# RWKV-7 scans of a two-layer trunk: 17 instead of 9 columns of each block inverse on VectorE, its second pair of copies on VectorE, and a new order of the parts around them

## The chip, the cores and the metric

One core of one Trainium2 chip runs the whole program. The metric is the device time in microseconds. The kernel before took 1643.92 us, the median of three runs (1643.02 to 1644.35).

## The reference, cut to what matters

The program computes two residual layers over 512 tokens of width 1024: layer 0 with windowed attention, layer 1 with RWKV-7 time mixing, each followed by a convolutional feed-forward network. The change touches the time mixing of layer 1 alone, of which the reference says:

```python
def step(state, inp):
    r_t, w_t, k_t, v_t, a_t, b_t = inp
    sa = jnp.einsum('bhvk,bhk->bhv', state, a_t)
    state = state * w_t[:, :, None, :] + sa[..., None] * b_t[:, :, None, :] + v_t[..., None] * k_t[:, :, None, :]
    y = jnp.einsum('bhvk,bhk->bhv', state, r_t)
    return state, y
...
y = y_f + y_b                       # a forward and a backward scan
mean = jnp.mean(y, axis=-1, keepdims=True)
var = jnp.mean(jnp.square(y - mean), axis=-1, keepdims=True)
yn = ((y - mean) * lax.rsqrt(var + RWKV_GN_EPS)).reshape(b, s, d) * lnx_w + lnx_b
out = (yn + (bonus_f + bonus_b).reshape(b, s, d)) * g
```

There are 16 heads of 64 channels. The kernel does the scans in 8 chunks of 64 tokens, and inside a chunk it needs the inverse of a triangular 64x64 matrix for each head, direction and chunk.

## The kernel before, in words

The heads go in 8 pairs (`ct`, 0 to 7). Before the scans' own stretch the projections write each pair's operands to DRAM (`ars`, `bks`, ...). `run` (line 1209 on) then goes through i = -1 to 7, and in each i through 8 chunks j. At each j it writes down the parts that the string `K.between[j]` (line 1314) names, in that order: `c` is the scan step of pair i, and the other letters are parts for pairs ahead of it or behind it (`PARTS`, line 1188). At the end every instruction is tied to the one written before it on its engine, so that each engine's order is the order in which the parts stand in these strings. Each engine takes its instructions strictly in that order, and what one instruction waits for also holds those behind it.

What one pair needs, and which letters stand for it:

- `l0` to `l3` (`low`): matmuls, then a masked copy on VectorE (L936) into `bw`, for pair i+2. `b0` and `b1` (`blocks`): the 32x32 diagonal blocks go to DRAM (`ls`, two DMAs for each direction, L942, queue SP), and with `b1` they all come back as the tile X (L947, two DMAs).
- `G`, `V`, `g`, `v` with a number n (`go`, which advances `solve`): n more of the 31 columns of the inverse of these blocks, for pair i+2 (capitals) or i+1 (small letters). A column is a product (`tg` or `tv`, L997) and an addition into Y (L999); G and g put both on GpSimd (POOL), V and v on VectorE (DVE). Each column reads the ones before it, so they follow each other whatever engine they are on. Columns run from 31 down to 1, with 31 elements in a partition at first, 136 in the middle (column 17) and 16 at the end.
- After column 1, the 32nd advance copies Y into a tile Z in two orders, `z1` (a transposed one, two copies) and `z0` (two copies), and three DMAs on ACT's queue store them to `zs`: two for z1 and one for z0. Z and X are taken from one ring of four tiles (`block`).
- `I` (`inverses`), pair i+1: `zs` comes back as `t32` and `tt` (six DMAs on SP). `L0`, `L1` (`level`) complete the inverses; `L1` ends in four small copies into `tt`.
- `t`, `a`, `x`, `m`, `u`, `w`: transposes, products, loads of the values. `m` ends in the tiles `mt` and `qt` (L1080, L1081 on DVE).
- `n0` to `n4` (`head_norm`) for pair i-1: `n1` has a power on POOL (L1142, `rv`), `n2` is one multiplication (L1144), `n3` transposes on PE, and `n4` is two operations of 512 elements on DVE (L1152 and L1153), the second of which also multiplies by the gate `gt`. Then the result is stored (`os`, L1157). `e` loads `gt` and `bo`, `p` loads a later pair's `bk` and `ar`.

Before the change a pair's 31 columns stand as 4 on POOL (j3), 5 and 4 on DVE (j4, j5), 4 and 4 on POOL (j6, j7), and, in the next i, 5 and 5 on POOL (j0, j1) with the copies. The first pair is inverted by POOL alone inside the projections, and seven pairs are left for this scheme.

A DMA signals one of eight semaphores, DMAHW0 to DMAHW7. They are given out in turn to the DMAs of both queues together, in the order in which the program was put down, and a DMA is not issued before the DMA eight places earlier, on the same semaphore, has landed. Below, this is called its lane.

Of the kernel before, what the change touches and what calls it, by code (L numbers as in the profile page):

```python
# [16 lines left out]
P = 128  # L17
# [5 lines left out]
HD = 64  # L23
# [792 lines left out]
def rwkv_scan(K, A, sc, mid):  # L816
# [4 lines left out]
    V = nc.vector  # L821
# [25 lines left out]
    def mk(shape, name, bufs=1, dt=F32):  # L847
        pool = mid if name in MID else pools[next((k for k, v in PLACE.items() if name in v), "batch")]
        return pool.tile(shape, dt, name=name, tag=name, bufs=bufs)
# [47 lines left out]
    def eng(name, i=0):  # L897
        x = K.eng.get(f"{name}/{K.ct}", K.eng[name])
        return {"V": V, "G": G, "C": C, "A": nc.any, "S": nc.sync}[x[i % len(x)]]

    def copy(name, i, out, in_):
        e = eng(name, i)
        if e is C:
            C.copy(out=out, in_=in_)  # L904
        else:
            e.tensor_copy(out=out, in_=in_)
# [72 lines left out]
    def block():  # L979
        R.nX += 1  # L980
        return R.Xs[R.nX % len(R.Xs)]

    def solve(ct, c):


        X = c.X
        Y = mk([P, 32, 16], f"Y{ct % K.ny}")
        Yf = Y.rearrange("p i j -> p (i j)")
        G.memset(Y, 0.0)
        G.memset(Yf[0:HD, 0::33], 1.0)  # L990
        G.memset(Yf[HD:P, 16::33], 1.0)
        for kx in range(31, 0, -1):
            en, nm = (G, "tg") if c.by == "G" else (V, "tv")
            m = kx // 2
            n = 16 - m
            tm = mk([P, 256], nm, 1)[:, 0:kx * n].rearrange("p (i j) -> p i j", j=n)
            en.tensor_tensor(out=tm, in0=X[:, 0:kx, kx:kx + 1].broadcast_to([P, kx, n]),  # L997
                             in1=Y[:, kx:kx + 1, m:16].broadcast_to([P, kx, n]), op=ALU.mult)
            en.tensor_tensor(out=Y[:, 0:kx, m:16], in0=Y[:, 0:kx, m:16], in1=tm, op=ALU.add)  # L999
            yield  # L1000
        Z = block()
        for h in range(2):
            yh = Y[HD * h:HD * h + HD]
            copy("z1", h, Z[HD:P].rearrange("p (j h) i -> p j h i", h=2)[:, :, h], yh.rearrange("p i j -> p j i"))
        for h in range(2):
            yh = Y[HD * h:HD * h + HD]
            copy("z0", h, Z[0:HD].rearrange("p i (j h) -> p i j h", h=2)[:, :, :, h], yh)
        zd = sc["z"][ct]
        for d in range(2):
            nc.scalar.dma_start(out=zd[0, 48 * d:48 * d + 16], in_=Z[HD + 48 * d:HD + 48 * d + 16])  # L1010
        nc.scalar.dma_start(out=zd[1], in_=Z[0:HD])

    def go(ct, c, n, by):

        c.by = by
        if not hasattr(c, "solving"):
            c.solving = solve(ct, c)
        for _ in range(n):
            next(c.solving, None)
# [241 lines left out]
def body(ctx, tc, A, out, stage=9):  # L1261
    nc = tc.nc
    K = Ctx()
# [46 lines left out]
    K.eng.update({"w": "VC", "bkt": "C", "bkt/0": "C", "x1": "C", "xa": "C", "xv": "C", "z1": "C", "Q": "C"})  # L1310
    K.begin, K.tail = (2,), ("pl", "", "", "")
    K.ny = 2
    K.eng["tt"] = "CV"
    K.between = ("w0 c l0 l1 b0 u g5", "c l2 l3 g6 b1 I", "c m1 w1 n0 e", "c t0 t1 n1 G4", "c a0 p V5 n2", "c L0 n3 V4", "c L1 a1 n4 G4", "c x0 x1 m0 G4")
    const = ctx.enter_context(tc.tile_pool(name="const", bufs=1, reuse_waits="tile"))

    @contextmanager
# [54 lines left out]
    def ffn(layer, xT, st, nxt, nst, store):  # L1372
# [4 lines left out]
    sc = {"ar": dram.tile([KT, 2, P, 2, NC, HD], F32, name="ars"), "bk": dram.tile([KT, 2, P, NC, 2, HD], F32, name="bks"),  # L1377
          "v": dram.tile([S, D], F32, name="vs"), "g": dram.tile([KT, P, S], F32, name="gs"),
          "bo": dram.tile([KT, P, S], F32, name="bos"), "o": dram.tile([KT, P, S], F32, name="os"),
          "l": dram.tile([KT, 2, 2, NC, 2, 32, 32], F32, name="ls"), "z": dram.tile([KT, 2, HD, 32, 32], F32, name="zs")}  # L1380
# [22 lines left out]
    with ExitStack() as end:  # L1403
# [25 lines left out]
        for ot, (hi, lo) in enumerate(ahead(K, [(A["wo"][i], n * P, nc.vector) for i in range(KT)])):  # L1429
            ps = scan.bank()  # L1430
            for kt in range(n):
                c = slice(kt * P, (kt + 1) * P)
# [4 lines left out]
        with tc.tile_pool(name="act2", bufs=1, reuse_waits="tile") as K.act:  # L1437
            K.accp = K.work = K.act
            on_tile = residual(xT, "nch1" if stage > 2 else None, st if stage > 2 else None, out if stage == 2 else None)
            for ot in range(KT):  # L1440
                ps = scan.bank()
                c = slice(ot * P, (ot + 1) * P)
# [82 lines left out]
```

## Time and profile before

| | us |
|---|---|
| median of three runs | 1643.92 |
| profiled execution, its own time | 1642.19 |
| span of that execution in the trace | 1640.4 |
| stretch of the scans, about | 907 to 1180 |
| PE busy in the span | 1476.3 (90%) |
| DVE busy | 1006.3 (61%) |
| ACT busy | 683.5 (42%) |
| POOL busy | 491.8 (30%) |

The shares are means over stages with different limits. PE is full in the attention and in both feed-forward networks; in the scans it is not. A timeline row gives start, length, engine, line, operation, tiles with their sizes, and in brackets the idle time of the engine ahead of it with what ended it. `xN` says that N instructions were merged into a row. Start times count from the beginning of the span.

### The profile page before, as it was taken

What the parts mean: (1) busy time and instruction counts of PE and PEld (TensorE: products, weight loads), DVE (VectorE), ACT (ScalarE), POOL (GpSimd) and SP (SyncE); (2) the same over time, 40 slices, a digit from 0 to 9 for tenths busy, and PEclk for the clock granted to TensorE, in tenths of its full rate; (3) what the DMA queues carried; (4) which work ended last, traced back from release to release, by engine and by line L of the source; (5) the groups of instructions that cost most, each with busy time, mean ns of one, the idle gap of its engine ahead of it and who ended that gap; (6) DMA issues with size and microseconds to landing.
All of it is one profiled execution on the core that took longest, in us unless ns stands there. A gap on an engine that the chain in (4) does not pass through costs nothing. (4 is left out here: it accounts for less than half of the span.)

```text
span 1640.4 us, 28397 instructions
## 1 busy us (share of the span) xinstructions
PE 1476.3 (90%) x11612; PEld 1191.6 (73%) x11612; DVE 1006.3 (61%) x1570; ACT 683.5 (42%) x1131; POOL 491.8 (30%) x645
## 2 busy tenths in 40 slices
PE   8999999999999998989975867667769999999999
PEld 7767688888888886667754756556647788888887
DVE  6876448777763349959886444555356677777222
ACT  5576434444432224665534333333423444444211
POOL 2630012223300016435696444444300233222000
PEclk9999999999999999999975687888979999999999
DMA  5200032332233322356546356554443232333341
GB/s 190 78 21 1 27 90 90 103 101 92 91 115 100 119 78 90 100 156 246 189 158 183 121 122 135 149 143 88 116 144 97 74 94 90 103 101 91 105 119 61
DMA packets 108978, 179.09 MB, mean 109 GB/s; under 512 B 49200, under 2 KB 62128, under 8 KB 108848
## 3 DMA queue, kind: packets, MB, share of 16 engines
q1 hardware_dynamic: 107552, 174.13, 35.0%
q10 hardware_dynamic: 1296, 3.15, 0.9%
q8 instruction: 91, 1.49, 0.4%
q14 instruction: 39, 0.32, 0.1%
HBM read 142.91 MB, written 34.34 MB: 108 GB/s over the span
## 5 line engine op out<-in xcount | busy, mean ns | idle before, releaser
L68 ACT CAST whi<-wraw 128x1024 fp32r<-128x1024 f32 (+2 forms) x196 | 200.3, 1023 | 270.5 <-PE mm L105 182.1
L104 PE MATMUL mm<-hl,whi 128*128 128x512 f32 x720 | 281.7, 391 | 1.5 <-DVE xT L1355 0.9
L106 PE MATMUL mm<-hl,wlo 128*128 128x512 f32 x720 | 281.6, 391 | 0.5 <-POOL wlo L71 0.4
L105 PE MATMUL mm<-hl,whi 128*128 128x512 f32 x720 | 281.4, 391 | 0.4 <-DVE hl L92 0.4
L71 DVE TENSOR_TENSOR wlo<-wraw,whi 128x1024 fp32r<-128x1024 f32 (+2 forms) x139 | 167.7, 1207 | 182.6 <-ACT whi L68 181.8
L71 POOL TENSOR_TENSOR wlo<-wraw,whi 128x1024 fp32r<-128x1024 f32 x57 | 137.0, 2404 | 414.4 <-ACT whi L68 414.4
L185 DVE SCALAR_TENSOR_TENSOR conv<-upad,par,conv 128x512 f32<-128x512 f32 x88 | 125.6, 1429 | 64.0 <-ACT conv L182 64.0
L106 PEld LDWEIGHTS mm<-hl,wlo 128*128 128x128 f32 x720 | 135.6, 188 | 31.9 <-POOL wlo L71 2.7
L104 PEld LDWEIGHTS mm<-hl,whi 128*128 128x128 f32 x720 | 135.8, 189 | 29.6 <-ACT hl L91 1.3
L105 PEld LDWEIGHTS mm<-hl,whi 128*128 128x128 f32 x720 | 135.8, 189 | 29.5 <-DVE hl L92 1.1
L106 PE MATMUL mm<-gh,wlo 128*128 128x512 f32 x352 | 139.0, 395 | 0.0
L104 PE MATMUL mm<-gh,whi 128*128 128x512 f32 x352 | 139.0, 395 | 0.0
L105 PE MATMUL mm<-gl,whi 128*128 128x512 f32 x352 | 139.0, 395 | 0.0
L997 POOL TENSOR_TENSOR tg<-X,Y 128x56 f32<-128x56 f32 (+20 forms) x185 | 70.4, 381 | 93.4 <-DVE Y L999 42.8
L97 ACT CAST gh<-gact 128x512 fp32r<-128x512 f32 x44 | 27.3, 621 | 141.4 <-DVE gact L194 141.4
L999 POOL TENSOR_TENSOR Y<-Y,tg 128x56 f32<-128x56 f32 (+20 forms) x185 | 77.6, 420 | 13.3
L182 ACT ACTIVATE conv<-upad,par 128x512 f32<-128x512 f32 x88 | 71.6, 815 | 21.5 <-DVE upad L180 21.3
L105 PEld LDWEIGHTS mm<-gl,whi 128*128 128x128 f32 x352 | 66.1, 188 | 16.1
L106 PEld LDWEIGHTS mm<-gh,wlo 128*128 128x128 f32 x352 | 66.1, 188 | 16.0
L104 PEld LDWEIGHTS mm<-gh,whi 128*128 128x128 f32 x352 | 66.1, 188 | 16.0
L187 DVE SCALAR_TENSOR_TENSOR conv<-upad,par,conv 128x512 f32<-128x512 f32 x88 | 70.1, 798 | 3.0
L192 ACT ACTIVATE silu<-conv 128x512 f32<-128x512 f32 x44 | 27.8, 632 | 91.2 <-DVE conv L187 91.2
(336 smaller groups left out, 3068.8 us busy)
## 6 DMA issues: line engine op xcount, KB each, us to landing
wraw<-in_w_up_dram SPq DMA_DIRECT2D x88, 512.0 KB, 3.6
wraw<-in_w_down_dram SPq DMA_DIRECT2D x32, 512.0 KB, 3.5
ars<-tab SPq DMA_DIRECT2D x16, 512.0 KB, 2.9
bks<-tab SPq DMA_DIRECT2D x16, 512.0 KB, 3.5
ar<-ars SPq DMA_DIRECT2D x8, 1024.0 KB, 8.4
bk<-bks SPq DMA_DIRECT2D x8, 1024.0 KB, 6.7
wraw<-in_w_down_dram SPq DMA_DIRECT2D x16, 384.0 KB, 3.1
wraw<-in_w_qkv_dram SPq DMA_DIRECT2D x11, 512.0 KB, 4.1
```

The costliest lines, as they stand in the source:

```text
L68: nc.scalar.copy(out=hi, in_=raw)
L71: lo_engine.tensor_tensor(out=lo, in0=raw, in1=hi.bitcast(F32), op=ALU.subtract)
L97: K.nc.scalar.copy(out=hi, in_=src)
L104: nc.tensor.matmul(ps, lhsT=lhs[0], rhs=rhs[0], start=first, stop=False)
L105: nc.tensor.matmul(ps, lhsT=lhs[0], rhs=rhs[1], start=False, stop=False)
L106: nc.tensor.matmul(ps, lhsT=lhs[1], rhs=rhs[0], start=False, stop=last)
L182: nc.scalar.activation(out=c, in_=u[:, 1:S + 1], func=AF.Identity, scale=K.par[:, cw + 2 * FT + ch:cw + 2 * FT + ch + 1], bias=K.par[:, cb ...
L185: nc.vector.scalar_tensor_tensor(out=c, in0=u[:, 0:S], scalar=K.par[:, cw + ch:cw + ch + 1], in1=c, op0=ALU.mult, op1=ALU.add)
L187: nc.vector.scalar_tensor_tensor(out=c, in0=u[:, 2:S + 2], scalar=K.par[:, cw + 4 * FT + ch:cw + 4 * FT + ch + 1], in1=c, op0=ALU.mult, op ...
L192: nc.scalar.activation(out=sg, in_=acts[0], func=AF.Silu)
L997: en.tensor_tensor(out=tm, in0=X[:, 0:kx, kx:kx + 1].broadcast_to([P, kx, n]), in1=Y[:, kx:kx + 1, m:16].broadcast_to([P, kx, n]), op=ALU. ...
L999: en.tensor_tensor(out=Y[:, 0:kx, m:16], in0=Y[:, 0:kx, m:16], in1=tm, op=ALU.add)
```

## The change

Three things change:

- `solve` takes a tile for z1, makes its two copies and issues their two stores, and only then takes a further tile for z0. z0's copies move from ACT to DVE (`K.eng["z0"]`).
- The override that gave every second one of the four `tt` copies of `L1` to DVE goes, and all four are on ACT.
- The strings of `K.between` change: `b1` stands ahead of the part that ends the inverse of pair i+1; the columns of a pair are now 3 on POOL (j3), 6, 6 and 5 on DVE (j4 to j6), 4 on POOL (j7), and 4 and 4 on POOL in the next i; and `n2`, `n3` and `n4` stand ahead of the columns of their chunk.

```diff
+        zd = sc["z"][ct]
         Z = block()
         for h in range(2):
-            yh = Y[HD * h:HD * h + HD]
-            copy("z1", h, Z[HD:P].rearrange("p (j h) i -> p j h i", h=2)[:, :, h], yh.rearrange("p i j -> p j i"))
-        for h in range(2):
-            yh = Y[HD * h:HD * h + HD]
-            copy("z0", h, Z[0:HD].rearrange("p i (j h) -> p i j h", h=2)[:, :, :, h], yh)
-        zd = sc["z"][ct]
+            copy("z1", h, Z[HD:P].rearrange("p (j h) i -> p j h i", h=2)[:, :, h], Y[er(h)].rearrange("p i j -> p j i"))
         for d in range(2):
             nc.scalar.dma_start(out=zd[0, 48 * d:48 * d + 16], in_=Z[HD + 48 * d:HD + 48 * d + 16])
+        Z = block()
+        for h in range(2):
+            copy("z0", h, Z[0:HD].rearrange("p i (j h) -> p i j h", h=2)[:, :, :, h], Y[er(h)])
         nc.scalar.dma_start(out=zd[1], in_=Z[0:HD])
...
-    K.eng["tt"] = "CV"
-    K.between = ("w0 c l0 l1 b0 u g5", "c l2 l3 g6 b1 I", "c m1 w1 n0 e", "c t0 t1 n1 G4", "c a0 p V5 n2", "c L0 n3 V4", "c L1 a1 n4 G4", "c x0 x1 m0 G4")
+    K.eng["z0"] = "V"
+    K.between = ("w0 c l0 l1 b0 u g4", "c l2 l3 b1 g4 I", "c m1 w1 n0 e", "c t0 t1 n1 G3", "c a0 p n2 V6", "c L0 n3 V6", "c L1 a1 n4 V5", "c x0 x1 m0 G4")
```

Lines from 1011 on stand one line higher after the change (L1144 becomes L1143), and the stores of z1 stand at L1006 instead of L1010.

Which lane each store takes is in the order of the two programs. At the end of the inverse of one pair (i = 1; the others are like it), ACT's queue has before, from the first copy of z1 to the square of the norm:

```order
L904 COPY X1_7484<-Y1_8643 64x16x32
L904 COPY X1_7484<-Y1_8643 64x512 [waits DMAHW4_49]
L904 COPY X1_7484<-Y1_8643 64x512
L1010 DMA zs_78<-X1_7484 16x1024 [waits DMAHW5_49,Activation_49]
L1010 DMA zs_78<-X1_7484 16x1024 [waits DMAHW6_49]
L1011 DMA zs_78<-X1_7484 64x1024 [waits DMAHW7_49,Activation_49]
L1137 ACTIVATE t_9180<-t_9178 128x512 [waits DVE_49]
```

The copies of z0 (64x512) are the second kind, and the stores hold lanes 5, 6 and 7. After the change the same place on ACT reads:

```order
L904 COPY X0_5953<-Y1_8643 64x16x32
L1006 DMA zs_78<-X0_5953 16x1024 [waits DMAHW5_49,Activation_49]
L1006 DMA zs_78<-X0_5953 16x1024 [waits DMAHW6_49]
L1010 DMA zs_78<-X1_7484 64x1024 [waits DMAHW6_49,DMAHW4_49,DVE_49]
L1136 ACTIVATE t_9180<-t_9178 128x512 [waits DVE_49]
```

The stores of z1 hold lanes 5 and 6, and the store of z0 waits for DVE's copies and takes lane 6 after the second of them. SP's queue at the same place, before, with the blocks of the next pair (L942), its values (L955) and X (L947):

```order
L942 DMA ls_77<-bw1_7305 32x16x32 [waits DMAHW0_49,DVE_49]
L942 DMA ls_77<-bw1_7305 32x16x32 [waits DMAHW1_49]
L955 DMA vv_9037<-vs_73 64x8x128 [waits DMAHW2_49,PE_49,Activation_49]
L955 DMA vv_9037<-vs_73 64x4x128 [waits DMAHW3_49]
L955 DMA vv_9037<-vs_73 64x4x128 [waits DMAHW4_49]
L942 DMA ls_77<-bw1_7305 32x16x32 [waits DMAHW5_49,DVE_49]
L942 DMA ls_77<-bw1_7305 32x16x32 [waits DMAHW6_49]
L947 DMA X2_7485<-ls_77 64x1024 [waits DMAHW5_49,DMAHW6_49,DMAHW1_49,DMAHW7_49,DMAHW0_49,Pool_49]
```

And the same piece of SP's queue after the change:

```order
L942 DMA ls_77<-bw1_7305 32x16x32 [waits DMAHW7_49,DVE_49]
L942 DMA ls_77<-bw1_7305 32x16x32 [waits DMAHW0_49]
L955 DMA vv_9046<-vs_73 64x8x128 [waits DMAHW1_49,PE_49,Activation_49]
L955 DMA vv_9046<-vs_73 64x4x128 [waits DMAHW2_49]
L955 DMA vv_9046<-vs_73 64x4x128 [waits DMAHW3_49]
L942 DMA ls_77<-bw1_7305 32x16x32 [waits DMAHW4_49,DVE_49]
L942 DMA ls_77<-bw1_7305 32x16x32 [waits DMAHW5_49]
L947 DMA X3_7486<-ls_77 64x1024 [waits DMAHW5_49,DMAHW7_49,DMAHW4_49,DMAHW0_49]
```

The last two stores of blocks waited for lanes 5 and 6 and X for lane 7, which are the three stores to `zs`; now the first of the two is on lane 4, the second is still on lane 5, and X waits for no store of `zs`.

On DVE, the end of a pair's columns (j5 and j6) before, where `st` is the scan step:

```order
L999 TENSOR_TENSOR Y_9241<-Y_9241,tv 128x19x7
L1115 TENSOR_TENSOR st<-bank,gc 128x128
L906 COPY tt_7307<-mm 32x8x32 x2
L1152 SCALAR_TENSOR_TENSOR t<-bank,par,bo 128x512
L1153 TENSOR_TENSOR t<-t,gt 128x512
L1080 TENSOR_TENSOR mt_9502<-mm,id_5026 128x4x64
```

and the same place after:

```order
L999 TENSOR_TENSOR Y_9241<-Y_9241,tv 128x17x8
L1114 TENSOR_TENSOR st<-bank,gc 128x128
L1151 SCALAR_TENSOR_TENSOR t<-bank,par,bo 128x512
L1152 TENSOR_TENSOR t<-t,gt 128x512
L997 TENSOR_TENSOR tv<-X_7486,Y_9241 128x128
L999 TENSOR_TENSOR Y_9241<-Y_9241,tv 128x16x8
L997 TENSOR_TENSOR tv<-X_7486,Y_9241 128x135
```

The `tt` copies are gone from DVE, and the two operations of `n4`, which stood behind DVE's last column, now stand between its 12th and its 13th. At the change of pairs (j1) the copies of z0 now stand on DVE between the last masks and the scan step:

```order
L936 TENSOR_TENSOR bw_7483<-pre_5949,mask 128x4x128
L936 TENSOR_TENSOR bw_7483<-mm,mask 128x4x128 x2
L906 COPY X_5953<-Y_9241 64x512 x2
L1114 TENSOR_TENSOR st<-bank,gc 128x128
L1079 TENSOR_TENSOR mt_9536<-pre_5948,id_5026 128x4x64
```

Before, the scan step followed the masks directly. PE's order is the same in both programs.

## Rows read from the trace of the kernel before

**Rows 1.** Stretch: us, busy PE, PEld, DVE, ACT, POOL (count), granted clock, DMA share, GB/s.

```profile
1040.00:1080.00 40.00, 27.68 (x798) 24.51 (x792) 21.20 (x56) 14.66 (x32) 19.63 (x52) 0.87 0.53 127
```

**Rows 2.** Timeline of POOL over one pair: start, length, line, operation, idle before.

```profile
1032.07 0.42 POOL L997 TENSOR_TENSOR tg<-X,Y 128x126 f32<-128x126 f32 x1 [6.30 <-DVE Y L999]
...
1039.59 0.41 POOL L997 TENSOR_TENSOR tg<-X,Y 128x121 f32<-128x121 f32 x1
...
1048.22 0.22 POOL L999 TENSOR_TENSOR Y<-Y,tg 128x16 f32<-128x16 f32 x1
...
1061.29 0.25 POOL L997 TENSOR_TENSOR tg<-X,Y 128x31 f32<-128x31 f32 x1 [4.65 <-DMA X<-ls]
...
1063.38 0.28 POOL L997 TENSOR_TENSOR tg<-X,Y 128x56 f32<-128x56 f32 x1
...
1070.33 0.43 POOL L997 TENSOR_TENSOR tg<-X,Y 128x126 f32<-128x126 f32 x1 [6.29 <-DVE Y L999]
```

**Rows 3.** Timeline of ACT at the same change of pairs.

```profile
1048.48 2.87 ACT L904 COPY X<-Y 64x512 f32<-64x512 f32 x3 [7.18 <-POOL Y L999]
1050.67 1.26 ACTq L1010 DMA_DIRECT2D zs<-X  x2
...
1052.53 0.63 ACT L1137 ACTIVATE t<-t 128x512 f32<-128x512 f32 x1 [0.53 <-ACT X L904]
```

**Rows 4.** Timeline of SP's DMA issues at the same change of pairs.

```profile
1053.08 0.90 SPq L942 DMA_DIRECT2D ls<-bw  x2
1055.96 1.57 SPq L947 DMA_DIRECT2D X<-ls  x2
```

**Rows 5.** What SP's queue waited for, 1000 to 1150 us: total, times, longest.

```profile
SPq L942 <- DMA zs<-X: 17.9, 5, 4.5
```

**Rows 6.** Timeline of DVE over the same pair.

```profile
1035.30 0.88 DVE L1153 TENSOR_TENSOR t<-t,gt 128x512 f32<-128x512 f32 x1
1040.29 0.42 DVE L1080 TENSOR_TENSOR mt<-mm,id 128x256 f32<-128x256 f32 x1 [4.12 <-PE mm L1077]
...
1047.01 1.28 DVE L936 TENSOR_TENSOR bw<-mm,mask 128x512 f32<-128x512 f32 x2
...
1064.07 0.24 DVE L997 TENSOR_TENSOR tv<-X,Y 128x81 f32<-128x81 f32 x1 [9.79 <-DMA gt<-gs]
...
1066.86 0.68 DVE L1144 TENSOR_TENSOR t<-t,rv 128x512 f32<-128x512 f32 x1
1067.46 0.28 DVE L1115 TENSOR_TENSOR st<-bank,gc 128x128 f32<-128x128 f32 x1
1067.66 0.26 DVE L997 TENSOR_TENSOR tv<-X,Y 128x110 f32<-128x110 f32 x1
...
1068.27 0.29 DVE L997 TENSOR_TENSOR tv<-X,Y 128x126 f32<-128x126 f32 x1
1068.59 0.29 DVE L999 TENSOR_TENSOR Y<-Y,tv 128x126 f32<-128x126 f32 x1
```

**Rows 7.** Timeline of POOL in the first two pairs of the scheme, first and last column.

```profile
908.45 0.25 POOL L997 TENSOR_TENSOR tg<-X,Y 128x31 f32<-128x31 f32 x1
...
932.64 0.22 POOL L999 TENSOR_TENSOR Y<-Y,tg 128x16 f32<-128x16 f32 x1
...
947.69 0.25 POOL L997 TENSOR_TENSOR tg<-X,Y 128x31 f32<-128x31 f32 x1 [14.02 <-DMA X<-ls]
...
971.99 0.22 POOL L999 TENSOR_TENSOR Y<-Y,tg 128x16 f32<-128x16 f32 x1
```

**Rows 8.** Timeline of DVE behind the last pair's inverse (i = 6).

```profile
1175.75 0.29 DVE L1115 TENSOR_TENSOR st<-bank,gc 128x128 f32<-128x128 f32 x1 [1.99 <-PE bank L1113]
...
1178.53 0.75 DVE L1152 SCALAR_TENSOR_TENSOR t<-bank,par,bo 128x512 f32<-128x512 f32 x1
1179.32 0.69 DVE L1153 TENSOR_TENSOR t<-t,gt 128x512 f32<-128x512 f32 x1
```

**Rows 9.** Groups of instructions by line: DVE's copies from SBUF to SBUF, 128x512.

```profile
L668 DVE COPY tf<-tnrm 128x512 f32<-128x512 f32 x8 | 3.9, 486 | 4.8 <-POOL tnrm L729 4.7
```

## The prediction

> **What bounds the kernel now.** I read the stretch's busy times first, then POOL's timeline over one pair, and then, at each end of POOL's work, the timeline of the engine or queue that goes on. In the scans no engine is full: of 40 us PE is busy 27.7, DVE 21.2, POOL 19.6 and ACT 14.7 [rows 1]. So something goes round in a chain, and it can be timed: POOL starts column 18 at 1032.07 in one pair and at 1070.33 in the next [rows 2]. The period is 38.26 us, and every part of it is one link:
>
> - POOL's 18 columns (18 to 1), 1032.07 to 1048.44: 16.37 [rows 2].
> - ACT makes the two copies of z1 and issues the first store to `zs` at 1050.67: 2.23 [rows 2, 3].
> - SP issues the blocks of the next pair (second direction) at 1053.08: 2.41 [rows 3, 4]. These blocks had long been ready, since the last mask that they need ended at 1048.29 [rows 6]. They waited for the store to `zs`: SP waited 17.9 us for it in five pairs [rows 5], and the order rows show why: they share its lane.
> - SP issues X at 1055.96, when both stores of blocks have landed: 2.88 [rows 4].
> - POOL starts the pair's first column at 1061.29: 5.33, of which it idled 4.65 for X alone [rows 2, 4].
> - POOL's four columns (31 to 28), to DVE's start at 1064.07: 2.78 [rows 2, 6].
> - DVE's nine columns (27 to 19), with a multiplication of the norm and one scan step between them, until POOL's 1070.33: 6.26 [rows 2, 6].
>
> These are 38.26 together. So the inverse of one pair and the blocks of the next are tied into a ring, though they need not be.
>
> **The change, part by part.** The sum is made on the profiled execution (1642.19, span 1640.4). The median is 1.73 above it, and I carry the difference over unchanged.
>
> *Does b1 leave ahead?* In part only. By the order rows of after the first of the two stores of blocks is off the lanes of `zs`, and X too, but the second is still on the lane of the first z1 store. The ring stays closed. The 2.23 and 2.41 stay. One store, not two, is issued between that wait and X. The two issues took 0.90 [rows 4], so half of it, 0.43 to 0.45, goes: 2.88 becomes 2.45. The 5.33 stays.
>
> *Columns.* POOL's first three end where the fourth started, 1063.38 - 1061.29 = 2.1 [rows 2]. Its last eleven run from 1039.59 to 1048.44: 8.85 [rows 2]. DVE's nine took 6.26, less 0.60 for the multiplication (1066.86 to 1067.46) and 0.20 for the step (1067.46 to 1067.66): 5.46, the hand-over to POOL included [rows 6]. New on DVE are eight. Column 28 (56 elements) costs about what the shortest seen, with 81, costs: 2 x 0.24 plus two gaps of 0.03, at most 0.55, and I take 0.5 [rows 6]. Columns 18 to 12 have 120 to 136 elements, and the product with 126 takes 0.29 and its addition starts 0.32 after it (1068.27), so a column is 0.65, and seven are 4.6 [rows 6]. The spread of 120 to 136 about 126 moves that by under 0.2. DVE's seventeen: 5.46 + 0.5 + 4.6 = 10.6. On POOL those eight cost 1039.59 - 1032.07 = 7.5 and 0.7, so 8.2 against 5.1 on DVE [rows 2].
>
> The rows thus say 1.6 to 1 for POOL against DVE at these sizes. The Trainium skill (GPSIMD Engine Reference, "Performance versus the Vector engine") gives 1.96 to 1 for an fp32 `tensor_tensor` of 2048 elements. By that ratio the eight columns would be an estimated 4.2 instead of 5.1 in each pair. The rows are of these very sizes, and I go by them; what a lower price would give is a rival below.
>
> *Norm ahead.* `n2` now stands ahead of all the columns, in the time in which DVE waits for X anyway: the 0.60 leaves the path. `n4` enters it, between DVE's 12th and 13th column. Its first operation starts 0.79 ahead of the second [rows 8]. The second took 0.88 with POOL busy beside it [rows 6] and 0.69 with POOL idle [rows 8]. POOL will be waiting for DVE there, so I take 0.69: 1.5 in all (1.7 at most). Two scan steps stand among the columns instead of one: 0.40.
>
> *z0 on DVE.* Two copies of 64x512. DVE's copy of 128x512 took 0.49 [rows 9], and ACT's z0 copies took 0.65 each (2.87 for three, 2.2 of them for z1) [rows 3], so 1.0 to 1.3 for both. They stand behind the last masks and hold the scan step, `m1` and `n0`. What hides them is the wait for X: POOL had 4.65 to spare there [rows 2]. ACT's square of the norm, started 4.1 after POOL's end [rows 2, 3], now waits in ACT's queue behind the z0 store, which waits for the second z1 store to land, issued some 0.6 after the first: 2.23 + 0.6 + 2.41 + 0.45 = 5.7 after POOL's end. So 1.6 and, by the earlier X, 0.43 go from the spare 4.65, and about 2.6 are left. z0 costs nothing on the path as long as that holds.
>
> *tt on ACT.* It takes DVE's two copies and the hand-overs out of the way of `n4`. ACT is busy 14.7 of 40, so nothing waits for it in the ring.
>
> *The sum.* A pair with all this (i = 1 to 5): 2.1 + 10.6 + 0.4 + 1.5 + 8.85 + 2.23 + 2.41 + 2.45 + 5.33 = 35.87, against 38.26: 2.4 saved, five times, 12.0. The first pair has neither steps nor norm in it and took 932.86 - 908.45 = 24.41 [rows 7]; it will take 2.1 + 10.6 + 8.85 = 21.55, so 2.9 less. The second has steps alone, 972.21 - 947.69 = 24.52 [rows 7], against 21.95, and 0.43 at the blocks: 3.0 less. After the last inverse nothing waits for X, and `n4` of i = 6 no longer stands behind the `tt` copies: it started at 1178.53 and could start after the step of 1175.75 [rows 8], between 0 and 2.6 earlier. z0's copies stand ahead of the step, so I take the middle, 1.5. Pair 0's z0 copies now stand in DVE's work in the projections, 0 to 1.3 later: 0.4. Total: 12.0 + 2.9 + 3.0 + 1.5 - 0.4 = 19.0. Behind the scans PE is full to the end, so all of it arrives there. 1642.19 - 19.0 = 1623.2, and on the scale of the median **1624.9 us**.
>
> **The rivals.**
>
> *The ring opens (1610).* The change then does what its words say: SP would have to get the second store of blocks out without the z1 store. For it: the blocks are ready 0.15 ahead of POOL's end [rows 2, 6]. Against it: the lanes in the order rows. X would come early, and the next to be late is POOL's own start, behind the norm's power: by the 2.6 above, 2.4 to 2.6 less for each of six pairs, some 15 us more: 1610.
>
> *Half of it (1634).* `n4` waits in front of DVE's last five columns for `gt` or `bo`, or the masks are late in some pairs. Against it: `n4` comes about ten us after X has landed. About half the gain would be left.
>
> *DVE's middle columns are cheaper (1619).* If the eight took 4.2 instead of 5.1, seven pairs would give another 6 us. Against it: 0.29 for the row with 126 elements, which is the mean of the new sizes [rows 6]. The ratio of the Trainium skill named above would do this.
>
> *The masks become the bound (1648, slower).* DVE's last columns now end later in the period than the chain over `tt`, `x0`, `x1` and `m0` can bear. Before, `m0` reached DVE at 1040.29, 8.2 after DVE's last column (1032.07, where POOL takes over), and the last mask ended 8.0 after that [rows 2, 6]. If this chain still starts where DVE's columns end, the last mask ends 16.2 after them, and POOL's end comes 8.9 after them, so 7.3 before that mask. The blocks then go at 7.3 instead of 2.23 + 2.41 = 4.6 after POOL's end, both of them after it: the period is 12.7 + 1.9 + 8.85 + 7.3 + 2.88 + 5.33 = 39.0, 0.7 above before, and with z0's copies at DVE behind the masks another 0.5 before POOL's power: 1.2 in six pairs, 7.2, less the first pair's 2.9 and a tail of nothing: some 4 above before, 1648. It decides where the last mask ends more than 4.6 after POOL's end. Against it: the scan step of j6 now stands ahead of `n4` and five columns (4.8 us), so PE gets on with `L1` and `x0` that much earlier, which puts the last mask at 7.3 - 4.8 = 2.5, 2.1 short of deciding.
>
> **How the numbers follow.** Forecast 0.75, with an own range of 1619 to 1630 (0.2 on seven columns, 0.2 on `n4`, 0 to 2.6 in the tail, 0.3 a pair on DMA landings); the ring opens 0.09; cheaper columns 0.02; half of it 0.08; masks 0.06. The range runs from 1611 to 1634: it takes in the forecast and the near parts of its neighbours. A measurement of this kernel can tell about 0.2% (3.3 us) from no change. Faster by more: 0.75 + 0.09 + 0.02 and 0.05 of the half = 0.91; within 0.2%: the other 0.03 and 0.01 of the masks = 0.04; slower: 0.05.
>
> **What would show it.** POOL's period between two first columns at 35.9 (33 if the ring opens, 39 if the masks bound it); SP's wait of L942 for `zs` still there, once a pair, with one block store behind it; POOL's idle time ahead of a pair's first column still ended by X, about 2.5 to 4; DVE's tv and Y with 126 elements at 0.29; `n4` between DVE's columns at 1.5; the last mask some us ahead of the second store of blocks. The prediction is wrong if POOL's first column waits for the power or for a memset instead of X, if the second store of blocks waits for DVE, or if the landing of X (5.33) changes with what is now in flight beside it.

## The result, and the profile after

The changed kernel took 1627.32 us (median of four runs, 1626.07 to 1627.81), the kernel before beside it 1643.66: a ratio of 0.9899, 95% interval 0.9882 to 0.9917. The forecast was 1624.9 with a range of 1611 to 1634. The span of the profiled execution fell from 1640.4 to 1625.7, by 14.7 us instead of the 19.0 of the sum; the medians fell by 16.3, since the profiled execution of before lies 1.5 us below its median and that of after 0.5 above. One term of the sum was far off, and smaller errors went the other way.

In the rows below the columns are start, length, engine (q: its queue), line, operation, tiles, and in brackets the idle time ahead with what ended it. POOL's timeline after, of the first pair's two ends and of one later pair, answers to [rows 2, 7]:

```profile
906.31 0.25 POOL L997 TENSOR_TENSOR tg<-X,Y 128x31 f32<-128x31 f32 x1
...
927.70 0.22 POOL L999 TENSOR_TENSOR Y<-Y,tg 128x16 f32<-128x16 f32 x1
...
946.05 0.25 POOL L997 TENSOR_TENSOR tg<-X,Y 128x31 f32<-128x31 f32 x1 [17.32 <-DMA X<-ls]
...
1040.57 0.22 POOL L999 TENSOR_TENSOR Y<-Y,tg 128x16 f32<-128x16 f32 x1
1049.41 1.65 POOL L1141 TENSOR_TENSOR rv<-rv,mhalf 128x8 f32<-128x8 f32 x1 [8.62 <-DVE rv L1140]
...
1054.00 0.25 POOL L997 TENSOR_TENSOR tg<-X,Y 128x31 f32<-128x31 f32 x1 [2.12 <-DMA X<-ls]
...
1068.25 0.41 POOL L997 TENSOR_TENSOR tg<-X,Y 128x121 f32<-128x121 f32 x1 [12.23 <-DVE Y L999]
...
1076.91 0.22 POOL L999 TENSOR_TENSOR Y<-Y,tg 128x16 f32<-128x16 f32 x1
```

From POOL's first column (1054.00) to its last (1077.13) is the phase of the columns, 23.13 us; from POOL's last (1040.79) to the next pair's first (1054.00) is what I call the turn, 13.21. Before, the same two were 25.42 and 12.85 (the end at 1048.44 and the first column at 1061.29 are in [rows 2]). The prediction did not add them up this way, but its legs fall into these two. Summed over the scans:

| us | before | after | difference | forecast |
|---|---|---|---|---|
| POOL's end of pair 0 (projections) | 883.52 | 882.45 | -1.07 | 0 |
| from there to the first column | 24.93 | 23.86 | -1.07 | +0.4 |
| columns of the first pair, the second | 24.41, 24.52 | 21.61, 21.73 | -2.80, -2.79 | -2.9, -2.57 |
| columns of five pairs | 127.11 | 115.64 | -11.47 | -9.9 |
| six turns | 79.39 | 84.60 | **+5.21** | **-2.6** |
| tail, to n4 of i = 6 and on to the end | | | -0.71 | -1.5 |

The first line is not counted as an effect of the edit: in all the runs here it lies between 882.1 and 884.7, without order.

Of the 5.21 the first turn has 3.30, and the five later ones have 1.91: in these X was issued 1.1 us later in all, and its own landing took 0.8 us more.

DVE after, in the same pair: its first column, the product with 126 elements, the step and n4, and, further on, n4 of i = 6 [rows 6, 8]:

```profile
1056.05 0.22 DVE L997 TENSOR_TENSOR tv<-X,Y 128x56 f32<-128x56 f32 x1 [4.26 <-POOL Y L999]
...
1062.10 0.29 DVE L997 TENSOR_TENSOR tv<-X,Y 128x126 f32<-128x126 f32 x1
1062.42 0.29 DVE L999 TENSOR_TENSOR Y<-Y,tv 128x126 f32<-128x126 f32 x1
...
1063.30 0.28 DVE L1114 TENSOR_TENSOR st<-bank,gc 128x128 f32<-128x128 f32 x1
1063.50 0.74 DVE L1151 SCALAR_TENSOR_TENSOR t<-bank,par,bo 128x512 f32<-128x512 f32 x1
1064.27 0.69 DVE L1152 TENSOR_TENSOR t<-t,gt 128x512 f32<-128x512 f32 x1
1064.88 0.28 DVE L997 TENSOR_TENSOR tv<-X,Y 128x128 f32<-128x128 f32 x1
...
1163.61 0.74 DVE L1151 SCALAR_TENSOR_TENSOR t<-bank,par,bo 128x512 f32<-128x512 f32 x1
```

The busy times of the same 40 us as in [rows 1] (PE, PEld, DVE, ACT, POOL, granted clock, DMA share, GB/s):

```profile
1040.00:1080.00 40.00, 32.91 (x865) 29.21 (x863) 27.91 (x79) 14.98 (x30) 11.87 (x35) 0.83 0.57 143
```

POOL is busy for 7.8 us less and DVE for 6.7 more. This is the direction of the change but not its exact size, since 40 us hold other parts of a period in the two runs. And the turn, on ACT's queue [rows 3], on SP's [rows 4], and SP's wait in the view of waits (total, times, longest) [rows 5]:

```profile
1043.03 0.78 ACTq L1006 DMA_DIRECT2D zs<-X  x2
1047.27 0.46 ACTq L1010 DMA_DIRECT2D zs<-X  x1
1047.78 0.63 ACT L1136 ACTIVATE t<-t 128x512 f32<-128x512 f32 x1 [4.78 <-DMA zs<-X]
```

```profile
1040.17 1.94 SPq L955 DMA_DIRECT2D vv<-vs  x3
1042.21 5.14 SPq L942 DMA_DIRECT2D ls<-bw  x2
1049.06 1.12 SPq L947 DMA_DIRECT2D X<-ls  x2
```

```profile
SPq L942 <- DMA zs<-X: 13.8, 4, 4.3
```

SP issued the first of the two last stores of blocks at 1042.21, as the lanes allow, and then stood before the second until z1's store of 1043.03 had landed. From that store to X it took 6.03 us, where the forecast had 2.41 + 2.45 = 4.86. What changed in this turn is the landing. The DMA issues over one turn (KB each, median us from issue to landing), of before:

```profile
vv<-vs SPq DMA_DIRECT2D x2, 128.0 KB, 4.4
zs<-X ACTq DMA_DIRECT2D x1, 256.0 KB, 3.0
zs<-X ACTq DMA_DIRECT2D x2, 64.0 KB, 2.4
```

and of after:

```profile
vv<-vs SPq DMA_DIRECT2D x2, 128.0 KB, 4.4
zs<-X ACTq DMA_DIRECT2D x1, 256.0 KB, 2.9
zs<-X ACTq DMA_DIRECT2D x2, 64.0 KB, 3.9
```

The stores of z1 (64 KB) now land 3.9 us after issue instead of 2.4. In before the values (vv, 0.5 MB) had been issued by 1048.50, 2.2 us ahead of z1's store at 1050.67; in after by 1042.11, 0.9 ahead of 1043.03. Their row in before:

```profile
1046.56 1.94 SPq L955 DMA_DIRECT2D vv<-vs  x3
```

The first turn is another case. DVE's first `mt` and the last masks (L936) of this turn, before:

```profile
928.38 0.42 DVE L1080 TENSOR_TENSOR mt<-pre,id 128x256 f32<-128x256 f32 x1 [9.82 <-PE pre L1077]
...
935.09 1.28 DVE L936 TENSOR_TENSOR bw<-pre,mask 128x512 f32<-128x512 f32 x2
```

and after:

```profile
926.95 0.42 DVE L1079 TENSOR_TENSOR mt<-pre,id 128x256 f32<-128x256 f32 x1 [8.05 <-PE pre L1076]
...
933.66 1.28 DVE L936 TENSOR_TENSOR bw<-pre,mask 128x512 f32<-128x512 f32 x2
```

Here DVE waits for PE, and the masks end 8.0 us behind the start of `mt` in both. From the pair's first column to `mt` it is 19.9 us before and 20.6 after, of which PE is busy 16.5 and 17.1, at a granted clock of 0.52 and 0.51, about the lower of its two levels (1.2 GHz). In all fourteen kernels of this document this time is 19.3 to 20.8, whether DVE does 9, 13 or 17 columns. Over the columns of all seven pairs and their turns the granted clock was 0.82 before and 0.78 after; what that costs no run here separates.

### The profile page after: what moved, and what is told of

It reads as the page before. It is cut to its first block, busy times and chain, and to the rows that moved or that the text cites. A ratio compares the mean times of both kernels' runs of the same rounds, so it can differ in the third digit from the quotient of the medians.

```text
span 1625.7 us, 28414 instructions
## 1 busy us (share of the span) xinstructions
PE 1488.2 (92%) x11612; PEld 1203.1 (74%) x11612; DVE 1035.8 (64%) x1682; ACT 679.4 (42%) x1131; POOL 442.4 (27%) x533
## 4 chain that ended last, share of the span: by engine, by line
PE 66%; DVE 14%; POOL 7%; DMA 6%; issue 4%; ACT 3%; SPq 0%; ACTq 0%; POOLq 0%; DVEq 0%
PE mm L104 16%; PE mm L105 16%; PE mm L106 16%; POOL Y L999 3%; POOL tg L997 2%; PE mm L387 2%; DMA X<-ls 2%; PE sc L104 2%; DVE tv L997 2%; DVE Y L999 2%; PE sc L105 2%; PE sc L106 2%; PE tp L382 2%; DVE wlo L71 1%; DMA zs<-X 1%
## 5 line engine op out<-in xcount | busy, mean ns | idle before, releaser
L997 POOL TENSOR_TENSOR tg<-X,Y 128x56 f32<-128x56 f32 (+16 forms) x129 | 46.4, 360 | 121.7 <-DVE Y L999 82.7
L106 PE MATMUL mm<-sx,wlo 128*128 128x512 f32 (+1 forms) x144 | 59.1, 410 | 2.9 <-DVE wlo L71 2.9
```

Of the source, the lines that this page charges most:

```text
L106: nc.tensor.matmul(ps, lhsT=lhs[1], rhs=rhs[0], start=False, stop=last)
```

## The experiments

The theories at the outset: (A) the turn became longer because the values are now in flight when z1's stores go, (B) because of the order of stores itself, (C) because DVE's columns make the masks late. Each run stands beside the kernel before on the same chip, which took 1643.1 to 1644.5 us there; differences between two runs are between medians that can come from two chips. Where columns and turns are given they are of POOL's timeline, as above.

**The values behind X.**

```diff
-"w0 c l0 l1 b0 u g4", "c l2 l3 b1 g4 I", ...
+"w0 c l0 l1 b0 g4", "c l2 l3 b1 g4 I u", ...
```

> The change, with the loads of the values (L955, three DMAs, 0.5 MB) put down behind X and the loads of the inverse instead of between the two pairs of block stores. Theory: the turn between two pairs got longer because the values are now in flight right ahead of the stores of z1 and of the blocks (those of z1 land 3.9 us after issue instead of 2.4), and because the second store of blocks still has the lane of the first z1 store. Both go: this order gives the block stores lanes of transfers that landed long ago. X then goes when z1's store has landed, 1043.0 + 2.4 = 1045.5 instead of 1049.06: 3.5 us less in each of six turns, 21 us, about 1606 us; stores of z1 back at 2.4. Rival: the stores slow each other and the values have no part: z1 still lands after 3.9, X at 1046.9, 2.1 less in six turns, about 1614. Second rival: the norm's power on POOL or the masks are late next, under 1 us a turn: 1621 or above.

Measured: 1652.79, ratio 1.0061 (1.0046 to 1.0076), slower than before. Of what was expected only the landing of z1's stores came, after 2.0 instead of 3.9. What waits in this kernel over 1000 to 1140 (total, times, longest):

```profile
PE pre L975 <- DMA vv<-vs: 14.0, 2, 7.9
...
DVE mt L1079 <- PE pre L1076: 10.4, 2, 5.3
```

The values come too late for PE, whose queue holds the scan steps behind L975; DVE's columns and masks are held in turn (the columns of pairs 3 to 7 25.3 to 26.9, the last mask 3.1 to 4.3 us behind POOL's end). The run says where the values may not go. The landing is as A has it, but what that is worth in the turns is hidden here, so it decides nothing between A and B.

**The columns alone**, on the kernel before:

```diff
-"... b0 u g5", "c l2 l3 g6 b1 I", ... "c t0 t1 n1 G4", "c a0 p V5 n2", "c L0 n3 V4", "c L1 a1 n4 G4", ...
+"... b0 u g4", "c l2 l3 g4 b1 I", ... "c t0 t1 n1 G3", "c a0 p V6 n2", "c L0 n3 V6", "c L1 a1 V5 n4", ...
```

> The kernel before, with 17 instead of 9 columns on DVE (3 on POOL, 6, 6 and 5 on DVE, 4 on POOL, then 4 and 4) and nothing else of the change; the norm's parts stay behind the columns, z0 and every second tt copy where they were. Theory: the columns are the whole gain, and the rest of the change made the turns longer. Eight columns save 2.8 us in the first two pairs and 2.7 in five (n4 is not on the path here): 5.6 + 13.5 = 19, with turns as before, so 1643.7 - 19 = about 1625, as fast as the whole change or faster. Rival: the columns make the turns longer, because DVE hands POOL its columns late and the next pair's masks come later (n4 and the tt copies stand behind them): turns 2 us longer each, 1636 or above.

Measured: 1642.20, ratio 0.9991 (0.9981 to 1.0): no change. The rival is nearer. The five full pairs' columns take 24.1 instead of 25.4, and the first three turns are 2.7, 2.8 and 1.8 longer. Half of the columns' gain is missing at DVE, where the `tt` copies stand ahead of its last five columns:

```profile
1074.50 0.42 DVE L906 COPY tt<-pre 32x256 f32<-32x256 f32 x1
1075.35 0.43 DVE L906 COPY tt<-pre 32x256 f32<-32x256 f32 x1 [0.43 <-ACT tt L904]
```

The turns grow with the order of stores of before, so B is not needed for it; the next run decides on B. But A is not all of it either. In the second and third turn the values had landed before the last blocks were issued, z1's stores took 2.5 and 2.9 us, and it is the second store of blocks that landed after 4.8 and 4.3 instead of 2.8 and 2.5. Why, no run shows.

**The columns undone**, all else of the change kept (`g5`, `g6`, `G4`, `n2 V5`, `n3 V4`, `n4 G4`):

> The change with the columns as before it (9 on DVE); the order of stores, z0 on DVE, tt on ACT and n2 ahead of the columns stay. Theory: the order of the stores makes the turns longer, whatever the columns: turns as in the whole change, columns 25.4 less 0.6 for n2 in five pairs, start and tail as in the whole change: 1643.7 + 5.2 - 3.0 - 3.1 = about 1643, no gain over the kernel before. Rival: the shorter columns made the turns longer, so here the turns go back to before's: 1643.7 - 3.0 - 3.1 = about 1637.5.

Measured: 1631.63, ratio 0.9932 (0.9918 to 0.9947), below both. The turns are not those of after but shorter than before's (14.22, 12.00, 12.43, 11.49, 11.30, 11.62: 6.3 less in all), and five pairs' columns are 24.8, 0.6 less, which is `n2`. Theory B falls here: with the new order of stores and the old columns the turns are shorter. The order, the norm, z0 and the `tt` copies together gave 12 of the change's 16 us, and the columns only 4, though they shortened their phase by 14.0 against this run: the turns took back 11.5. One turn of it, at SP, and then the landing of z1's stores in it:

```profile
1043.17 1.94 SPq L955 DMA_DIRECT2D vv<-vs  x3
1045.21 4.95 SPq L942 DMA_DIRECT2D ls<-bw  x2
1051.82 1.11 SPq L947 DMA_DIRECT2D X<-ls  x2
```

```profile
zs<-X ACTq DMA_DIRECT2D x2, 64.0 KB, 2.3
```

Its lanes are those of after, but z1's store went at 1047.48, 2.4 us behind the last issue of values, and X followed after 4.34 instead of 6.03.

**b1 behind the columns again** (`"c l2 l3 b1 g4 I"` to `"c l2 l3 g4 b1 I"`):

> The change with the blocks' part b1 put back behind the last columns in j1; all else stays. Theory: what freed the first of the two block stores is that z0's store is put down later, not b1's place; the lanes are the same in this order, so the time is that of the whole change, 1627 within 1.5. Rival: b1's place is what freed it: the 0.43 us of a store's issue comes back in six turns, or the store waits for z1's second store too, 1630 to 1633.

Measured: 1627.61, ratio 0.9904 (0.9882 to 0.9925), as the change. The place of b1 has no effect that can be told (the six turns take 83.96 us against 84.60); the theory held.

**The values first in j0:**

```diff
-"w0 c l0 l1 b0 u g4", ...
+"w0 u c l0 l1 b0 g4", ...
```

> The change, with the loads of the values put down first in j0, ahead of the blocks of the first direction: they can go about 1035.5 instead of 1040.2, so they have landed before z1's stores (1043.0), and the matmuls that read the values (L975), for which the run with the values behind X waited up to 7.9 us, get them early. The block stores get lanes of transfers that landed long ago; X's second half has the lane of z1's first store. Theory (the values in flight delay the landing of z1 and of the blocks, and the lane adds to it): z1 lands 2.4 us after issue, X goes at the later of that and of the blocks, about 4.7 us behind POOL's last column instead of 8.2; of these 3.5 us POOL's power and memset (2 to 2.9 us of spare, moving 1 to 2 earlier themselves) let 2.5 to 3.5 through; in the first turn the blocks land 2.4 instead of 4.9 after issue. Six turns: 15 to 21 less, 1607 to 1612 us. Rival (the turn is bound by the masks or by POOL's power, both of which come late because DVE does more columns): under 1 us a turn, 1621 or above. Rival (z1 lands late whatever is in flight): 3.9 us stays, 2 a turn, about 1615.

Measured: 1617.04, ratio 0.9829 (0.9800 to 0.9858), 10 us below the change; its four runs lie between 1609.8 and 1619.6. SP's queue and its waits:

```profile
1026.57 1.97 SPq L955 DMA_DIRECT2D vv<-vs  x3
1038.51 3.62 SPq L942 DMA_DIRECT2D ls<-bw  x4
1045.46 1.11 SPq L947 DMA_DIRECT2D X<-ls  x2
```

```profile
SPq L942 <- DVE bw L936: 6.4, 4, 1.8
```

The wait of L942 for `zs` is gone, z1's stores land after 2.0 to 3.0, and the four later turns are 10.30, 12.19, 10.45 and 11.64. That is the theory, but less than it by 5 to 10 us, since now the rival (C) begins: the last mask comes 2.0 to 2.9 us behind POOL's end and X waits for the blocks behind it. The second turn (13.50) is that of after, with the last mask 4.0 behind POOL's end. In the first (17.37) the mask comes 6.8 behind POOL's end, 7.0 in after. There X left 2.1 us earlier, 4.3 behind the mask instead of 6.2, but its second half landed after 5.6 instead of 4.3, and of the turn only 0.8 was gained.

**n4 behind the columns** (`"c L1 a1 n4 V5"` to `"c L1 a1 V5 n4"`):

> The change with n4 (two operations on DVE, L1151 and L1152) behind DVE's last five columns instead of ahead of them. Theory: n4 costs the columns 1.38 us in five pairs; behind them it fills part of the 1.42 us in which DVE then waits for PE; the masks come no more than 0.2 later. The columns get 6.9 us shorter in all; but POOL's end comes 1.4 nearer to the loads of the values, whose landing beside z1's stores made the turns longer, so the turns grow again by up to 1.4 each: 1620 to 1627, and the landing of z1's stores over 3.9. Rival: no such interplay, the turns stay at 13.3: 1620.4. Second rival: the masks come 1.4 later, and X with them: 1627 with z1's landing unchanged.

Measured: 1622.93, ratio 0.9875 (0.9855 to 0.9896). The columns took 22.05, 1.08 less (1.38 was expected); and the turns grew by 1.0 in all. The worst is 15.18, where z1's stores were issued 0.15 us ahead of the end of the values' issue; their landing there:

```profile
zs<-X ACTq DMA_DIRECT2D x2, 64.0 KB, 4.4
```

The landing speaks for the theory (2.7 to 4.4 in the five later turns); the time alone does not tell it from the rival's 1620.4, which the interval (1619.6 to 1626.4) still holds.

**tt on both engines** (`K.eng["tt"] = "CV"` again):

> The change with every second tt copy back on DVE. Theory: in the run with the columns alone two copies and the wait between them stood for 1.3 us ahead of DVE's last five columns (their phase took 24.1 instead of 23.1 with n4 in it, 22.9 instead of 21.6 without); the same here: 1.3 more in each of the first pair and of pairs 3 to 7, 7.6 in all, and POOL's end farther from the loads of the values, which gives back part in the turn: 1629 to 1635. Rival: the copies fill time in which DVE waits anyway: 1627 within 1.5.

Measured: 1633.24, ratio 0.9930 (0.9909 to 0.9951). The five pairs' columns took 24.6, 1.46 more, and the later turns 11.38 to 12.51, with z1 landing after 2.4 to 2.7. As expected: later at the turn, and a shorter turn.

**z0 on ACT** (`K.eng["z0"] = "C"`):

> The change with z0's copies on ACT again (z1's stores are still issued ahead of them). Theory: z0 on DVE costs nothing in the pairs, since the z0 store waits for its lane (z1's second store) longer than for either engine; only the start gains from it, about 1.1 us (pair 0's z0 copies out of ACT's way): 1627 to 1629. Rival: z0's 0.85 us on DVE holds the scan step and with it the norm and POOL's power, which is close behind X: 1622 to 1625. Rival: z0 behind z1 on ACT holds the square of the norm: 1630 or above.

Measured: 1636.22, ratio 0.9951 (0.9933 to 0.9968). My theory missed. The rival at 1630 or above has the time but not the cause: POOL's power starts 6.6 to 7.5 us behind POOL's end, earlier than in after (7.9 to 8.6), and X still ends POOL's wait, of 4.0 to 4.8 us in the five later turns. SP's queue in one turn:

```profile
1043.52 1.94 SPq L955 DMA_DIRECT2D vv<-vs  x3
1050.36 1.28 SPq L942 DMA_DIRECT2D ls<-bw  x2
1053.45 1.11 SPq L947 DMA_DIRECT2D X<-ls  x2
```

Both stores of blocks stand again until z1's have landed (issued at 1046.76): with z0 on ACT its store takes the lane right behind z1's, which moves all that follow by one, as before the change. The lanes do not follow the strings here. In the traces of before and of this run z1, z1 and z0 hold the three lanes ahead of the next pair's first blocks, which the strings name earlier; in after z0's comes only behind the last blocks. What sets this order no run shows. But z0's engine is all that differs from after, so it is what freed the first of these stores. The start is back at 24.85, so its 1.07 were z0's too; the six turns are 2.4 longer than after's, and the rest behind the last column 1.0. That is 4.4 of the 6.1 us between the two spans, and pair 0's end, which wanders, 1.6; the medians lie 8.9 apart, and the last 2.8 of them I cannot place.

**A quarter of the values' bytes**, lanes and order as in the change:

```diff
+        k = P if ct < 3 else P // 4
...
-nc.sync.dma_start(out=c.VV[...], in_=vs[:, at(d, q):at(d, q) + n])
+nc.sync.dma_start(out=c.VV[...][:, :, 0:k], in_=vs[:, at(d, q):at(d, q) + n, 0:k])
...
+nc.scalar.copy(out=c.VV[...][:, :, k:], in_=K.ident[...])
```

> The change with its order and its lanes as they are, but from pair 3 on the loads of the values bring a quarter of the bytes (32 of 128 columns, 0.125 instead of 0.5 MB); ACT fills the rest with a constant in time in which it idles, so the scans of pairs 3 to 7 compute something else. Theory (the values in flight delay the landing of z1's stores): z1 lands 2.4 to 2.8 us after issue in those turns instead of 3.9, X comes 1.1 to 1.5 earlier in each of four or five turns, POOL's spare of 2 allows it: 1619.5 to 1623, and the turns there at 11.5 to 12.2 as in the run with the columns undone. Rival (the distance from the values is only a by-product; the stores of the first blocks or the state of z0 delay the landing): 3.9 stays and 1627 within 1.5.

Measured: 1621.22, ratio 0.9876 (0.9858 to 0.9894), 6 us below the change. The four turns with fewer bytes took 11.36, 12.02, 12.07 and 12.85 against 13.29, 13.21, 12.70 and 13.81: 4.7 less. In one of them SP's queue, and the DMA issues:

```profile
1037.83 1.94 SPq L956 DMA_DIRECT2D vv<-vs  x3
1039.87 4.32 SPq L942 DMA_DIRECT2D ls<-bw  x2
1045.81 1.37 SPq L947 DMA_DIRECT2D X<-ls  x2
```

```profile
zs<-X ACTq DMA_DIRECT2D x2, 64.0 KB, 2.8
vv<-vs SPq DMA_DIRECT2D x1, 64.0 KB, 2.4
```

z1's stores are about as near to the values as in after, 1.4 us behind in this turn and 0.4 ahead to 1.4 behind in the four, and land after 2.0 to 2.8. The clearest is the turn with the stores 0.4 us ahead of the end of the values' issue, at 2.0: with all the bytes, ten turns within 1 us of it and with the same pace of issue took 2.9 to 4.4. This is theory A, with lanes and order unmoved. About 1.9 of the 6 us lie behind POOL's last column and are not explained by it.

**Values first and n4 behind** (both edits above):

> Both of the two edits that made the change faster: the values first, and n4 behind DVE's last columns. Theory (with the values first the masks are what X waits for, 2 to 3 us behind POOL's end; they hang on the steps and matmuls of j5 to j7, not on POOL): n4 moves into time in which DVE waits for PE's products (3 to 4 us ahead of mt), the columns get 1.05 shorter in five pairs, and the masks come when they came: POOL's end moves ahead and the turn grows by as much: 1617 within 2. Rival (the masks follow DVE's columns, so they come earlier too): 5 us less, about 1612.

Measured: 1616.26, ratio 0.9838 (0.9823 to 0.9853). As expected, no gain over the values first alone that can be told: the columns took 22.04, 1.05 less, and the four later turns (12.84, 12.70, 10.34, 11.18) 2.5 more in all.

**The kernel before with the values first:**

```diff
-"w0 c l0 l1 b0 u g5", ...
+"w0 u c l0 l1 b0 g5", ...
```

> The kernel before, with one letter moved: the values first in j0, nothing of the change. The lanes turn so that no store of blocks waits for a store to zs; only X's second half has the lane of z1's first store. Theory: the ring between the inverse and the blocks was the price of before: X goes 4.7 us behind POOL's end instead of 7.5, and POOL has 4.2 to 4.9 to spare: 2.4 to 2.8 less in five or six turns, about 1628, as much as the whole change. Rival (the masks, which end with POOL's last column, and their blocks' landing hold X): 1.5 a turn, about 1635. Rival (no gain: power and memset come next): 1641 or above.

Measured: 1625.97, ratio 0.9907 (0.9887 to 0.9926): one letter of the string is worth as much as the whole change. The five later turns are 8.77 to 9.92 instead of 12.4 to 13.4. X leaves when the stores of blocks have landed, 4.2 us behind POOL's end (1040.65) in this pair, and in two of the five its second half then stands until z1's first store has landed. On SP's queue and on POOL:

```profile
1044.89 1.11 SPq L947 DMA_DIRECT2D X<-ls  x2
```

```profile
1049.86 0.25 POOL L997 TENSOR_TENSOR tg<-X,Y 128x31 f32<-128x31 f32 x1 [1.02 <-DMA X<-ls]
```

**13 columns on DVE**, values first, n4 behind (`"w0 u c l0 l1 b0 g5", "c l2 l3 b1 g6 I"`, then `G3`, `n2 V5`, `n3 V4`, `V4 n4`, `G5`):

> The values first, n2 ahead and n4 behind the columns, and 13 instead of 17 columns on DVE (3 on POOL, 5, 4 and 4 on DVE, 5 on POOL, then 5 and 5). Theory: with the values first, X waits for the later of z1's store (4.2 to 4.7 us behind POOL's end, as in the kernel before with the values first) and of the blocks (about 4 behind the last mask); with 17 columns the mask is 3 to 4 us behind POOL's end, with 9 about level with it. With 13 DVE ends 2.6 us earlier in the period than in the run with the values first and n4 behind, so the mask comes about level with POOL's end, POOL's phase is 22.04 - 2.6 + 3.75 = 23.2 and the turn 9.2 to 9.7: a period of 32.4 to 32.9 against its 33.8: about 6 less than its 1616, 1608 to 1612. Rival (the masks do not follow DVE's columns, or the stores collide again): the turns stay at 10.3 to 12.8 and the time is 1616 or above.

Measured: 1613.18, ratio 0.9800 (0.9777 to 0.9823), the fastest. The columns take 23.5 and the last four turns 9.46, 9.80, 8.71 and 9.64, with the last mask from 0.3 us ahead of POOL's end to 1.4 behind it. The theory held for the turns; the median is 1 us above its range, and the first two turns (15.53, 11.36) stayed longer than it said.

## Why the prediction was right, step by step

- *Which chain.* Right: after the change too X ends POOL's wait ahead of the first column, in all six turns, in the five later ones with 1.90 to 2.91 us of idle time (about 2.6 were said to be left). POOL's period between two first columns was 35.8 to 36.9 there, where 35.9 was said. One reading was loose: the 17.9 us of SP's wait [rows 5] are five waits in four pairs and not five pairs. The sum does not use it.
- *Columns.* Right to 0.3 us a pair. The legs were 2.1 + 10.6 + 0.4 + 1.5 + 8.85 = 23.45; measured 23.13, with n4 at 1.38 (1063.50 to 1064.88) and DVE's 17 columns at 10.42 (12.20 from 1056.05 to 1068.25, less n4 and two steps). The product with 126 elements took the 0.29 of the row from before. `n2` was worth the 0.6 that was said, by the run with the columns undone. On the rate of the two engines: starts lie 0.48 apart on POOL with 121 elements and 0.32 on DVE with 120, 1.5 to 1. The Trainium skill's 1.96 to 1 (GPSIMD Engine Reference, "Performance versus the Vector engine"; 2048 elements) does not carry over to this size, and the measurement decides.
- *The turn.* **This is the term that was mis-sized**: -0.43 in each of six turns was forecast, and they grew by 5.21 in all. The step "the 2.23 and 2.41 stay" failed. The 2.41 was a landing time of before, and it was carried over to a place where 0.5 MB of values had come closer. The columns did it: they bring POOL's end, and with it z1's stores, nearer to the values, which follow the masks and did not move with POOL. Without the columns the six turns are 11.5 shorter than the change's (columns undone), and with a quarter of the bytes four turns are 4.7 shorter. The prediction named the neighbourhood of a transfer only for X, in its last sentence, and not for z1. X's 5.33 changed too: from its issue to POOL's first column it was 4.9 to 5.6 in the five later turns before, and 4.9 in three and 5.9 in two of them after. What lengthened these two no run shows. Of the 7.8 us by which the turns missed, these five have 4.1, and the first has 3.7 for another reason.
- *The first turn.* It grew by 3.30 alone. Here the masks bind after the change: the last of them ended 27.9 us behind the pair's first column before (936.37) and 28.6 after (934.94), so nothing of the 2.8 that the columns gained came through. They hang on PE's products, by the rows on `mt` above, and not on DVE's columns. X followed 6.2 behind the last mask in both, by two ways: before, the blocks stood 2.6 us for z1's landing and landed after 2.9; after, they went at once, right behind the values, and landed after 5.3. The prediction had treated this pair as the others. Moving the values gained 0.8 of it, and no run was made to change what PE does there.
- *b1.* The prediction said that one of the two stores comes off z1's lane, and that held. By its rows it did not say which edit does this; it is z0's move to DVE, not b1's place.
- *z0 and the start.* "Costs nothing as long as X covers it" held, since X still ended every wait. ACT's square, which waits behind the z0 store, started 7.0 us behind POOL's end (1047.78) instead of the 5.7 of the sum, because z1's stores landed later. The start was forecast at +0.4 and came at -1.07, which goes again with z0 on ACT.
- *The tail.* -1.5 was taken as the middle of 0 and 2.6; it was -0.7.
- *The rivals.* The ring did not open, for the reason given (the lane). Where it was opened, by the values' place, 10 us came instead of 15, and the masks were next, as the slower rival said of DVE's late columns. In the change itself they do not bind from the second pair on.

The errors cancelled in part: +7.8 in the turns and +0.8 in the tail against -1.7 in the columns, -1.5 at the start and -1.1 ahead of it, +4.3 in all. That the medians lie only 2.4 us from the forecast is in part luck: nothing ties these errors to each other, and the two profiled executions lie on opposite sides of their medians.

## What to carry to other kernels

When a stage is made shorter, list what is now in flight beside each transfer on the chain; a landing time read in the old place is a price of that place. Where DMAs share semaphores in turn, moving one load or one copy turns the lanes for all that follow, and that may be the largest effect of an edit whose words speak of something else. Shorten a chain on the engine that also feeds its rival only until the two ends meet: with the values first, 13 columns took 1613.2 us and 17 took 1616.3. The 1626.0 with 9 columns is no clean third point, since that run lacks the other edits.

## What the runs showed of the hardware

How late the two 64 KB stores of z1 land depends on what else is in flight, though it is on another queue: with a quarter of the values' bytes they land earlier. In the turns in which SP issued the three loads of values without a pause (1.95 us for 0.5 MB), the stores landed 2.3 to 2.8 us after issue where they went 1.7 us or more behind the last of these issues (eight turns of before, columns undone and tt on both), and 2.8 to 4.4 where they went between 1.4 us ahead and 1.7 behind (18 turns of seven kernels). With a quarter of the bytes they landed after 2.0 to 2.8 at the second distance (four turns). The distance is not all: in ten further turns between 0.9 us ahead and 1.2 behind, in which the three issues took 2.3 to 3.1 us, the stores landed after 2.0 to 3.0. And the values are not the only cause: in the last turn of the kernel before with the values first they had been issued 10 us earlier, and the stores landed after 3.7.

The Trainium skill (DMA: Bandwidth & Descriptors, "Latency and other measured facts") puts the access to DRAM at 0.2 us on average and 2 us at high load and calls it the main part of a transfer's fixed cost. The rows agree in size (1.5 to 2 us more beside the loads), but no run here tells whether it is that latency or the sharing of the DMA engines.
